# Expert steps for half-full positions: the turn of h and the gate's ScalarE and VectorE work moved to fixed places

## The chip, the cores and the metric

The kernel runs on one core of a Trainium2 chip. The metric is the device time of one execution in microseconds (us), the median of three runs. One execution was also recorded by the hardware profiler; the rows below are from that trace. Its engines are TensorE (PE, with its weight loads as PEld), VectorE (DVE), ScalarE (ACT), GpSimd (POOL) and SyncE (SP), which issues the loads from HBM.

## The reference

A two-layer encoder trunk on 256 tokens of width 1024, all in float32. The change lies in the last block of the second layer, a mixture of eight experts of which each token uses two:

```
def swiglu(xn, w_gu, w_down):
    g, u = jnp.split(xn @ w_gu, 2, axis=-1)
    return (jax.nn.silu(g) * u) @ w_down
...
    for e in range(N_EXPERTS):
        out = out + comb[..., e:e + 1] * swiglu(xn, w_gu[e], w_down[e])
```

An expert's inner width is 3584, so `w_gu` is 1024 x 7168 and `w_down` 3584 x 1024, for each of eight experts.

## The kernel before

The experts are handled one after the other in eight positions. Which expert stands in which position is decided on the chip by the number of its tokens. Positions 2, 4 and 6 (`NARROW`) take at most 64 tokens, the others up to 128. All positions read the same amount of weights.

A position has seven steps j, each for 512 columns of the inner width. A step works on chunks of weights of 128 x 2048 float32 (1.05 MB, one load each): two for the gate (g0, g1), two for the up product (u0, u1), and, from j = 1 on, two for the down product of the step before (d0, d1). Float32 is kept through a split: `split` (L168, L169) makes of a chunk a high part `hi` (a cast on ACT) and a rest `lo` (a subtraction on DVE, which reads `hi`), in two casts of 1024 columns per engine and chunk. `hi` and `lo` rotate through four tiles each, so a cast waits until PE has done with the tile of four casts earlier.

In a narrow position the 64 tokens' high and low parts stand side by side as the 128 columns that PE holds (`xg`, and `ht` for h), so a chunk needs eight matmuls (`narrow`, L1123): four with `hi`, four with `lo`. u1 is not split: four float32 matmuls on the raw chunk (L1139, eight records in the trace). The product then holds two halves of rows that must be added: `gate` copies them crosswise out of PSUM (ACT, L1156, L1157, tile `esg`), adds (DVE, L1158), applies silu (ACT, L1159) and multiplies by the up product (DVE, L1163, tile `eh`), which needs the last u1 matmul. `to_rows` then turns h by four matmuls (L1172, tile `ht`; "the turn" below) and splits it into the side-by-side form (`side_by_side`: ACT L1053, DVE L1054).

Each engine runs its own instructions in order. The order is made by a scheduler from the program's order and the times that it assumes; two instructions of one engine are tied by hand only where `tc.issue_after(ins)` stands. Loads are issued on SP's queue, each as soon as its buffer (11 of `raw`, 6 of `spare`) is free; nothing in the change touches their order.

Of the kernel before, what the change touches and what calls it, by code (L numbers as in the profile page):

```python
# [25 lines left out]
F32 = mybir.dt.float32  # L26
F32R = mybir.dt.float32r
I32 = mybir.dt.int32
AF = mybir.ActivationFunctionType
# [3 lines left out]
P = 128  # L33
D = 1024
KD = D // P
# [4 lines left out]
NE = 8  # L40
# [9 lines left out]
HALF = CAP // 2  # L50
# [31 lines left out]
def _build(ctx, tc, io, cap):  # L82
# [8 lines left out]
    w2b, w1b = 4, 5  # L91
# [8 lines left out]
    def f32(ap):  # L100
        return ap.bitcast(F32)
# [4 lines left out]
    def acc_tile(name="acc"):  # L106
        return psA.tile([P, 512], F32, tag="acc", name=name)
# [4 lines left out]
    def tr_tile(name="tr", dt=F32):  # L112
        return psT.tile([P, 512], dt, tag="tr", name=name)
# [33 lines left out]
            nc.sync.dma_start(raw[:, sl], ap[:, sl])  # L147
        return raw

    done = []  # L150

    def split(raw, n=CH, pieces=2, apart=()):

        cut = (n // 2 + P - 1) // P * P
        parts = []
        for a, b in ((0, cut), (cut, n)):
            if len(parts) in apart:  # L160
                both = rawp.tile([P, CH], F32R, tag="raw", name="apart")
                hi, lo = both[:, :CH // 2], both[:, CH // 2:]
            else:
                hi = hip.tile([P, CH // 2], F32R, tag="hi", name="hi")
                lo = lop.tile([P, CH // 2], F32R, tag="lo", name="lo")
            step = (b - a) * 2 // pieces
            for i in range(0, b - a, step):
                done[:] = (S.copy(hi[:, i:i + step], raw[:, a + i:a + i + step]),  # L168
                           V.tensor_sub(lo[:, i:i + step], raw[:, a + i:a + i + step],  # L169
                                        f32(hi[:, i:i + step])))  # L170
            parts.append((hi, lo))

        def at(a, b):
            hi, lo = parts[a >= cut]
            o = cut if a >= cut else 0
            return hi[:, a - o:b - o], lo[:, a - o:b - o]
        return at
# [620 lines left out]
    last = conv31(KD - 1)  # L798
# [250 lines left out]
    def side_by_side(dst, src):  # L1049

        v = dst.rearrange("p (k s n) -> p k s n", s=2, n=HALF)
        src = src.rearrange("p (k n) -> p k n", n=HALF)
        S.copy(v[:, :, 0, :], src)  # L1053
        V.tensor_sub(v[:, :, 1, :], src, f32(v[:, :, 0, :]))  # L1054

    class Gather:
# [20 lines left out]
        def rows_narrow(self):  # L1077
            px = tr_tile("gx")
            for k in range(KD):
                for t in range(2):  # L1080
                    PE.matmul(px[:, k * HALF:(k + 1) * HALF],
                              xt[:, t * D + k * P:t * D + (k + 1) * P],
                              self.oh[:, t, :HALF], start=t == 0, stop=t == 1)
            side_by_side(xg[:, :D], px)
# [25 lines left out]
    def whole_chunk():  # L1110
        if not ahead:
            fetch()
        return ahead.popleft()

    def chunk(pieces=2):
        return split(whole_chunk(), pieces=pieces)

    def narrow(ps, xs, ws, first, last):

        n = len(xs)  # L1120
        for part in range(2):
            for i, (x, w) in enumerate(zip(xs, ws)):
                ins = PE.matmul(ps, x, w[part], start=first and i == part == 0,  # L1123
                                stop=last and part == 1 and i == n - 1)
        return ins

    def expert(e, g, following):
        nonlocal fn
        py = out_tiles()
        two = e in NARROW  # L1130

        def gate_up(j, gu):
            pz = acc_tile("gu")
            for kh in range(2):
                xs = [xg[:, k * P:(k + 1) * P] for k in range(kh * 4, kh * 4 + 4)]
                if two and gu == kh == 1:
                    w = whole_chunk()
                    for kk in range(4):
                        PE.matmul(pz, f32(xs[kk]), w[:, kk * 512:(kk + 1) * 512],  # L1139
                                  start=False, stop=kk == 3)  # L1140
                    continue
                w = chunk()
                ws = [w(kk * 512, (kk + 1) * 512) for kk in range(4)]
                if two:
                    narrow(pz, xs, ws, kh == 0, kh == 1)
                    continue
                moving(pz, [(xg[:, k * P:(k + 1) * P], xg[:, D + k * P:D + (k + 1) * P])
                            for k in range(kh * 4, kh * 4 + 4)],
                       ws, kh == 0, kh == 1)
            return pz  # L1150

        def gate(pg, pu):
            sg = work.tile([P, 512], F32, tag="w2", name="esg", bufs=w2b)
            if two:

                S.copy(sg[:HALF], pg[HALF:])  # L1156
                S.copy(sg[HALF:], pg[:HALF])  # L1157
                V.tensor_add(sg, sg, pg)  # L1158
                S.activation(sg, sg, AF.Silu, scale=g.cw[:, 1:2])  # L1159
            else:  # L1160
                S.activation(sg, pg, AF.Silu, scale=g.cw[:, 1:2])
            h = work.tile([P, 512], F32, tag="w2", name="eh", bufs=w2b)
            V.scalar_tensor_tensor(h, pu, g.cw[:, 1:2], sg, op0=ALU.mult, op1=ALU.mult)  # L1163
            return h

        def to_rows(j, h):
            pt = tr_tile("ht")
            o = (j % 2) * D
            if two:

                for i in range(4):
                    PE.matmul(pt[:, i * HALF:(i + 1) * HALF], h[:, i * P:(i + 1) * P], both,  # L1172
                              start=True, stop=True)
                return side_by_side(ht[:, o:o + 512], pt[:, :4 * HALF])
            for i in range(4):
                PE.transpose(pt[:, i * P:(i + 1) * P], h[:, i * P:(i + 1) * P], ident)
            S.copy(ht[:, o:o + 512], pt)
            V.tensor_sub(ht[:, o + 512:o + D], pt, f32(ht[:, o:o + 512]))

        def down(j, n):  # L1180
            w = chunk(4 if e == NE - 1 and j == 6 else 2)
            o = (j % 2) * D
            if two:
                return narrow(py[n], [ht[:, o + f * P:o + (f + 1) * P] for f in range(4)],
                              [w(f * 512, (f + 1) * 512) for f in range(4)], j == 0, j == 6)
            return moving(py[n],
                   [(ht[:, o + f * P:o + (f + 1) * P], ht[:, o + 512 + f * P:o + 512 + (f + 1) * P])
                    for f in range(4)],
                   [w(f * 512, (f + 1) * 512) for f in range(4)], j == 0, j == 6)

        def weighted(n):
            src = py[n]
            hi, lo = (work.tile([P, 512], F32R, tag="w2", name=name, bufs=w2b) for name in ("yh", "yl"))
            S.activation(hi, src, AF.Copy, scale=g.cw[:, 0:1])
            done[:] = [V.scalar_tensor_tensor(lo, src, g.cw[:, 0:1], f32(hi),
                                              op0=ALU.mult, op1=ALU.subtract)]
            return hi, lo

        def scatter(n, y, tile=tr_tile):
            for t in range(2):  # L1200
                pz = tile("so")
                PE.matmul(pz, g.oT[:, t * P:(t + 1) * P], y[0], start=True, stop=False)
                PE.matmul(pz, g.oT[:, t * P:(t + 1) * P], y[1], start=False, stop=True)
                a = acc[:, t * D + n * 512:t * D + (n + 1) * 512]
                V.tensor_add(a, a, pz)  # L1205

        h = None
        for j in range(7):
            pg = gate_up(j, 0)
            if j:  # L1210
                to_rows(j - 1, h)
            pu = gate_up(j, 1)
            h = gate(pg, pu)
            if j:
                down(j - 1, 0)
                if j == 6:
                    to_rows(6, h)
                down(j - 1, 1)
            if following is not None and j in (3, 5):
                following.step(j)  # L1220
        if following is not None:
            following.rows()
        else:
            fn = big_tile("fn")
            nc.sync.dma_start(fn[:, :D], io["final_norm"].to_broadcast([P, D]))
        down(6, 0)
        y = weighted(0)
        last = down(6, 1)
        if following is not None:
            scatter(0, y)  # L1230
            scatter(1, weighted(1))
        else:
            y1 = weighted(1)
            with tc.issue_after(last.ins):
                scatter(0, y)
            scatter(1, y1, acc_tile)
# [268 lines left out]
```

## Time and profile before

| | us |
|---|---|
| median of 3 runs (lowest, highest) | 1547.98 (1547.81, 1549.23) |
| the profiled execution | 1547.42 |
| its span in the trace | 1545.7 |
| PE busy | 1511.9 |
| DVE busy | 1298.9 |
| ACT busy | 1052.1 |

The span is the time from the first to the last instruction; the execution's own time is 1.7 us more. Matmuls are pipelined: the record of a 128x512 matmul is 0.39 us long while the next one starts 0.23 us after it, so a busy PE can still have lost time.

### The profile page before, as it was taken

Reading aid. Unit: us, or ns where it says so; the run is one execution under the profiler, and the core shown is the slowest. Engines: PE = TensorE matmul, PEld = TensorE weight load, DVE = VectorE, ACT = ScalarE, POOL = GpSimd, SP = SyncE. Lnnn points to the kernel's source line nnn. Section 1 sums busy time; section 2 is a strip of 40 time slices with the busy share of each in tenths; the row PEclk is TensorE's granted clock in tenths of the full one; section 3 lists DMA queues with packets and bytes.
Section 4 is the critical chain, followed back from the end, with each engine's and each line's share of the span. In section 5 each row is a group of like instructions: output and inputs, shape, how many; then the busy total and the mean of one; then the engine's idle time right before and its main releaser. Section 6 shows DMA issues by size and latency. Waiting matters only on the chain.

```text
span 1545.7 us, 23643 instructions
## 1 busy us (share of the span) xinstructions
PE 1511.9 (98%) x8558; PEld 1294.3 (84%) x8558; DVE 1298.9 (84%) x1735; ACT 1052.1 (68%) x1381; POOL 148.1 (10%) x230
## 2 busy tenths in 40 slices
PE   8999999999999999999999999999999999999996
PEld 8899999999998998888888768888667888667885
DVE  7876677776898868999999989889889888889897
ACT  6555554455585647777777877777777777777775
POOL 4710100001394210000000000000000000000000
PEclk9999999999999999999999999999999999999998
DMA  9654454336536566998999999998999999999950
GB/s 370 269 191 164 142 186 166 120 113 236 188 134 244 174 264 221 371 377 334 373 366 342 397 422 412 381 375 331 403 402 376 367 361 343 408 392 382 364 191 30
DMA packets 65213, 451.42 MB, mean 292 GB/s; under 512 B 7360, under 2 KB 7488, under 8 KB 12480
## 3 DMA queue, kind: packets, MB, share of 16 engines
q1 hardware_dynamic: 65088, 449.83, 76.6%
q8 instruction: 69, 1.13, 0.3%
q14 instruction: 56, 0.46, 0.1%
HBM read 448.75 MB, written 1.05 MB: 291 GB/s over the span
## 4 chain that ended last, share of the span: by engine, by line
PE 82%; DVE 9%; POOL 3%; issue 3%; ACT 2%; DMA 1%; SPq 0%; DVEq 0%; POOLq 0%; ACTq 0%
PE gu L211 8%; PE gu L212 8%; PE gu L216 8%; PE acc L205 7%; PE acc L203 7%; PE acc L204 7%; DVE lo L169 6%; PE gu L1139 5%; PE gu L1123 4%; PE py L211 4%; PE py L216 4%; PE py L212 4%; PE py L1123 3%; POOL part L779 2%; PE gx L1042 1%
## 5 line engine op out<-in xcount | busy, mean ns | idle before, releaser
L169 DVE TENSOR_TENSOR lo<-raw,hi 128x1024 fp32r<-128x1024 f32 (+3 forms) x573 | 671.6, 1208 | 113.9 <-ACT hi L168 103.6
L168 ACT CAST hi<-raw 128x1024 fp32r<-128x1024 f32 (+3 forms) x573 | 565.4, 1030 | 212.9 <-PE acc L204 89.4
L169 DVE TENSOR_TENSOR lo<-spare,hi 128x1024 fp32r<-128x1024 f32 (+1 forms) x226 | 260.9, 1198 | 24.4 <-ACT hi L168 20.4
L168 ACT CAST hi<-spare 128x1024 fp32r<-128x1024 f32 (+1 forms) x226 | 221.5, 1035 | 23.6 <-PE gu L212 11.7
L211 PE MATMUL gu<-hi,xg 128*128 128x512 f32 x560 | 218.8, 391 | 0.0
L212 PE MATMUL gu<-hi,xg 128*128 128x512 f32 x560 | 218.3, 390 | 0.0
L216 PE MATMUL gu<-lo,xg 128*128 128x512 f32 x560 | 154.2, 391 | 0.6 <-DVE lo L169 0.6
L216 PEld LDWEIGHTS gu<-lo,xg 128*128 128x128 f32 x560 | 104.7, 188 | 23.9 <-DVE lo L169 1.9
L211 PEld LDWEIGHTS gu<-hi,xg 128*128 128x128 f32 x560 | 105.1, 188 | 22.2 <-ACT hi L168 0.2
L212 PEld LDWEIGHTS gu<-hi,xg 128*128 128x128 f32 x560 | 105.1, 188 | 21.8
L211 PE MATMUL py<-hi,ht 128*128 128x512 f32 x280 | 111.1, 398 | 0.0
L212 PE MATMUL py<-hi,ht 128*128 128x512 f32 x280 | 109.3, 390 | 0.0
L205 PE MATMUL acc<-a2h,lo 128*128 128x256 f32 x336 | 95.2, 283 | 0.0
L204 PE MATMUL acc<-a2l,hi 128*128 128x256 f32 x336 | 95.2, 283 | 0.0
L203 PE MATMUL acc<-a2h,hi 128*128 128x256 f32 x336 | 95.1, 283 | 0.0
L1401 POOL TENSOR_TENSOR fo<-accum,fn 128x512 f32<-128x512 f32 x2 | 2.5, 1272 | 948.9 <-DVE accum L1205 948.9
L1123 PE MATMUL gu<-lo,xg 128*128 128x512 f32 x252 | 80.4, 411 | 7.9 <-DVE lo L169 7.6
L216 PE MATMUL py<-lo,ht 128*128 128x512 f32 x280 | 84.0, 395 | 0.0
L1123 PE MATMUL gu<-hi,xg 128*128 128x512 f32 x252 | 71.3, 397 | 0.0
L1123 PEld LDWEIGHTS gu<-lo,xg 128*128 128x128 f32 x252 | 43.4, 188 | 31.5 <-DVE lo L169 25.2
L203 PEld LDWEIGHTS acc<-a2h,hi 128*128 128x128 f32 x336 | 64.5, 192 | 0.0
L205 PEld LDWEIGHTS acc<-a2h,lo 128*128 128x128 f32 x336 | 64.5, 192 | 0.0
(424 smaller groups left out, 3171.9 us busy)
## 6 DMA issues: line engine op xcount, KB each, us to landing
raw<-in_moe_gu SPq DMA_DIRECT2D x139, 1024.0 KB, 7.1
spare<-in_moe_gu SPq DMA_DIRECT2D x85, 1024.0 KB, 7.2
raw<-in_moe_down SPq DMA_DIRECT2D x78, 1024.0 KB, 7.4
spare<-in_moe_down SPq DMA_DIRECT2D x32, 1024.0 KB, 7.0
raw<-in_ffn_gu SPq DMA_DIRECT2D x22, 1024.0 KB, 4.8
raw<-in_pw SPq DMA_DIRECT2D x12, 1024.0 KB, 4.8
raw<-in_ffn_down SPq DMA_DIRECT2D x16, 704.0 KB, 4.1
raw<-in_wk SPq DMA_DIRECT2D x8, 1024.0 KB, 7.3
```

What stands on the lines that cost most here:

```text
L168: done[:] = (S.copy(hi[:, i:i + step], raw[:, a + i:a + i + step]), V.tensor_sub(lo[:, i:i + step], raw[:, a + i:a + i + step], f32(hi[:, ...
L169: V.tensor_sub(lo[:, i:i + step], raw[:, a + i:a + i + step], f32(hi[:, i:i + step])))
L203: PE.matmul(ps, a[0], b[0], start=first, stop=False)
L204: PE.matmul(ps, a[0], b[1], start=False, stop=False)
L205: PE.matmul(ps, a[1], b[0], start=False, stop=last)
L211: PE.matmul(ps, a[0], b[0], start=first and i == 0, stop=False)
L212: PE.matmul(ps, a[1], b[0], start=False, stop=False)
L216: ins = PE.matmul(ps, a[0], b[1], start=False, stop=last and i == n - 1)
L779: G.tensor_add(part, part, prod)
L1042: PE.matmul(px[:, kk * P:(kk + 1) * P], xt[:, t * D + d0:t * D + d0 + P], oh[:, t, :], start=t == 0, stop=t == 1)
L1123: ins = PE.matmul(ps, x, w[part], start=first and i == part == 0, stop=last and part == 1 and i == n - 1)
L1139: PE.matmul(pz, f32(xs[kk]), w[:, kk * 512:(kk + 1) * 512], start=False, stop=kk == 3)
```

## The change

For narrow positions a step is written out as a whole (`step_narrow`). The chunks are split in the order g0, g1, u0, d0, d1. The turn of the step before's h is tied behind g0's matmuls, and g1's matmuls behind the turn. The gate's copies and their sum (`fold`) are tied behind the last casts or the last but one, the silu and the multiplication behind the casts of d1; the split of the turned h behind the casts of u0. `casts` only records the ACT instructions to tie to. No instruction is added or taken away; wide positions keep their code.

```diff
-    done = []
+    done, casts = [], []
...
+                casts.append(done[0])
...
+        def step_narrow(j, h):
...
+            pg, pu = acc_tile("gu"), acc_tile("gu")
+            g0 = chunk()
+            g1 = chunk()
+            last = narrow(pg, xs[:4], parts(g0), True, False)
+            u0 = chunk()
+            if j:
+                with tc.issue_after(last.ins):
+                    pt, last = turn_narrow(j - 1, h)
+                with tc.issue_after(casts[-1].ins):
+                    rows_narrow(j - 1, pt)
+            with tc.issue_after(last.ins):
+                narrow(pg, xs[4:], parts(g1), False, True)
+            u1 = whole_chunk()
+            d0 = chunk() if j else None
+            narrow(pu, xs[:4], parts(u0), True, False)
+            d1 = chunk() if j else None
+            with tc.issue_after(casts[-2 if j else -1].ins):
+                sg = fold(pg)
+            for kk in range(4):
+                last = PE.matmul(pu, f32(xs[4 + kk]), u1[:, kk * 512:(kk + 1) * 512],
+                                 start=False, stop=kk == 3)
+            with tc.issue_after(casts[-1].ins):
+                h = gate(sg, pu)
+            if j:
+                down(j - 1, 0, d0)
+                down(j - 1, 1, d1)
+            return h
```

`turn_narrow` holds the four matmuls of the turn, `rows_narrow` the call of `side_by_side`, and `fold` the two copies and the sum that stood in `gate`.

The order that comes out, first on ACT, one step in the middle of position 4 before (the casts are those of d0 and d1 of the step before, then of g0, g1 and u0 of the next step):

```order
L1156 COPY esg<-gu 64x512
L1157 COPY esg<-gu 64x512
L1159 ACTIVATE esg<-esg,cw 128x512
L168 CAST hi<-spare 128x1024 x2
L168 CAST hi<-raw 128x1024 x2
L1053 CAST ht<-ht 128x4x64
L168 CAST hi<-raw 128x1024 x6
```

and now, from the casts of d0 and d1 on:

```order
L168 CAST hi<-spare 128x1024 x2
L168 CAST hi<-raw 128x1024 x2
L1146 COPY esg<-gu 64x512
L1147 COPY esg<-gu 64x512
L168 CAST hi<-raw 128x1024 x2
L1204 ACTIVATE esg<-esg,cw 128x512
L168 CAST hi<-raw 128x1024 x4
L1054 CAST ht<-ht 128x4x64
```

The copies and the silu stood ahead of the four casts of the down chunks; the copies now stand behind them, and the silu behind two casts more (those of the next step's g0).

DVE at the same place before; the two groups of four between `esg` and `ht` are the rests of d0 and d1, the six those of g0, g1 and u0:

```order
L1158 TENSOR_TENSOR esg<-esg,gu 128x512
L169 TENSOR_TENSOR lo<-spare,hi 128x1024
L1163 SCALAR_TENSOR_TENSOR eh<-gu,cw,esg 128x512
L169 TENSOR_TENSOR lo<-spare,hi 128x1024
L169 TENSOR_TENSOR lo<-raw,hi 128x1024 x2
L1054 TENSOR_TENSOR ht<-ht 128x4x64
L169 TENSOR_TENSOR lo<-raw,hi 128x1024 x6
```

and now:

```order
L1148 TENSOR_TENSOR esg<-esg,gu 128x512
L169 TENSOR_TENSOR lo<-raw,hi 128x1024 x2
L1206 SCALAR_TENSOR_TENSOR eh<-gu,cw,esg 128x512
L169 TENSOR_TENSOR lo<-raw,hi 128x1024 x4
L1055 TENSOR_TENSOR ht<-ht 128x4x64
L169 TENSOR_TENSOR lo<-spare,hi 128x1024 x2
L169 TENSOR_TENSOR lo<-raw,hi 128x1024 x2
```

The multiplication that makes h (`eh`) stood inside the four rests of d0 and d1; it now stands behind all four and behind the next step's two of g0.

PE in position 4 before, from the four u1 matmuls on, through d0 and d1 (`py`) and the next step's g0, g1 and u0:

```order
L1139 MATMUL gu<-spare,xg 128x512 x4
L1123 MATMUL py_11128<-hi,ht 128x512 x4
L1123 MATMUL py_11128<-lo,ht 128x512 x2
L1172 MATMUL ht<-kept,eh 128x64 x4
L1123 MATMUL py_11129<-hi,ht 128x512 x2
L1123 MATMUL py_11128<-lo,ht 128x512 x2
L1123 MATMUL py_11129<-hi,ht 128x512 x2
L1123 MATMUL py_11129<-lo,ht 128x512 x4
L1123 MATMUL gu<-hi,xg 128x512 x4
L1123 MATMUL gu<-lo,xg 128x512 x4
```

and now:

```order
L1193 MATMUL gu<-raw,xg 128x512 x4
L1124 MATMUL py_11129<-hi,ht 128x512 x4
L1124 MATMUL py_11129<-lo,ht 128x512 x4
L1124 MATMUL py_11130<-hi,ht 128x512 x4
L1124 MATMUL py_11130<-lo,ht 128x512 x4
L1124 MATMUL gu<-hi,xg 128x512 x4
L1124 MATMUL gu<-lo,xg 128x512 x4
L1155 MATMUL ht<-kept,eh 128x64 x4
L1124 MATMUL gu<-hi,xg 128x512 x4
L1124 MATMUL gu<-lo,xg 128x512 x4
```

The turn moved from 6 matmuls behind u1 to 24 behind it. At a narrow position's last step no g0 follows, and the turn stands straight behind the 16 matmuls of d0 and d1. The steps of positions 4 and 6 read alike, before and now.

## Rows read from the trace of the kernel before

**Rows 1.** The page, part 1: busy time, share of the span, instructions.

```profile
PE 1511.9 (98%) x8558; PEld 1294.3 (84%) x8558; DVE 1298.9 (84%) x1735; ACT 1052.1 (68%) x1381; POOL 148.1 (10%) x230
```

**Rows 2.** Timeline, PE: start, us, instruction; turns in positions 2, 4, 6.

```profile
862.53 1.00 PE L1172 MATMUL ht<-kept,eh 128*128 128x64 f32 x8
...
902.89 1.00 PE L1172 MATMUL ht<-kept,eh 128*128 128x64 f32 x8
...
1086.65 1.00 PE L1172 MATMUL ht<-kept,eh 128*128 128x64 f32 x8
...
1164.75 1.00 PE L1172 MATMUL ht<-kept,eh 128*128 128x64 f32 x8
...
1321.55 1.00 PE L1172 MATMUL ht<-kept,eh 128*128 128x64 f32 x8
...
1399.62 1.00 PE L1172 MATMUL ht<-kept,eh 128*128 128x64 f32 x8
```

**Rows 3.** Stretches from turn to turn: length, busy by engine, PEclk, DMA share, GB/s.

```profile
876.43:889.89 13.46, 13.46 (x58) 9.92 (x56) 13.06 (x14) 11.95 (x15) 0.00 (x0) 1.00 1.00 405
889.89:902.89 13.00, 13.00 (x56) 9.54 (x54) 12.97 (x14) 10.99 (x14) 0.00 (x0) 1.00 1.01 423
...
914.29:929.84 15.55, 14.70 (x57) 9.53 (x56) 13.11 (x14) 11.73 (x14) 0.00 (x0) 1.00 1.01 422
...
1102.21:1117.79 15.58, 14.72 (x58) 9.53 (x56) 13.13 (x14) 11.73 (x14) 0.00 (x0) 1.00 1.01 416
...
1133.33:1149.22 15.89, 15.18 (x64) 10.23 (x63) 13.31 (x15) 12.00 (x15) 0.00 (x0) 1.00 1.00 404
```

**Rows 4.** Timeline of ACT in position 4, a step; brackets: idle before, releaser.

```profile
1095.33 0.58 ACT L1156 COPY esg<-gu 64x512 f32<-64x512 f32 x1 [1.57 <-PE gu L1123]
...
1097.41 0.72 ACT L1159 ACTIVATE esg<-esg,cw 128x512 f32<-128x512 f32 x1 [0.91 <-DVE esg L1158]
1098.04 1.97 ACT L168 CAST hi<-spare 128x1024 fp32r<-128x1024 f32 x2
...
1103.51 5.79 ACT L168 CAST hi<-raw 128x1024 fp32r<-128x1024 f32 x6
```

**Rows 5.** Timeline of DVE in the same step of position 4.

```profile
1099.09 1.23 DVE L169 TENSOR_TENSOR lo<-spare,hi 128x1024 fp32r<-128x1024 f32 x1 [1.72 <-ACT hi L168]
1101.04 0.75 DVE L1163 SCALAR_TENSOR_TENSOR eh<-gu,cw,esg 128x512 f32<-128x512 f32 x1 [0.72 <-PE gu L1139]
1101.70 1.22 DVE L169 TENSOR_TENSOR lo<-spare,hi 128x1024 fp32r<-128x1024 f32 x1
...
1105.44 6.89 DVE L169 TENSOR_TENSOR lo<-raw,hi 128x1024 fp32r<-128x1024 f32 x6
```

**Rows 6.** Timeline of PE: position 4, and the wide position 3's first step.

```profile
1107.84 0.73 PE L1123 MATMUL gu<-lo,xg 128*128 128x512 f32 x2 [0.41 <-DVE lo L169]
...
1112.38 0.74 PE L1123 MATMUL gu<-lo,xg 128*128 128x512 f32 x2 [0.16 <-DVE lo L169]
1112.96 3.60 PE L1139 MATMUL gu<-raw,xg 128*128 128x512 f32 x8
1116.00 1.49 PE L1123 MATMUL py<-hi,ht 128*128 128x512 f32 x4
...
950.24 0.73 PE L216 MATMUL gu<-lo,xg 128*128 128x512 f32 x2 [0.19 <-DVE lo L169]
```

**Rows 7.** The chain in order of time, position 2: start, us, what.

```profile
855.13 3.43 PE gu L1139 x8
858.56 3.67 PE py L1123 x16
...
862.69 0.84 PE ht L1172 x8
```

**Rows 8.** SP's waits (total, times, longest), and loads' us from issue to landing, 830 to 940.

```profile
SPq L147 <- DVE lo L169: 835.4, 307, 14.6
...
DMA to landing us min/median/max: 4.7/12.5/14.3
```

More of the change, by code (lines that the diff above doesn't have):

```diff
@@ L1134, in gate_up @@
             for kh in range(2):
[L1135 to L1141, printed above, removed]
                 w = chunk()
                 ws = [w(kk * 512, (kk + 1) * 512) for kk in range(4)]
-                if two:
-                    narrow(pz, xs, ws, kh == 0, kh == 1)
-                    continue
                 moving(pz, [(xg[:, k * P:(k + 1) * P], xg[:, D + k * P:D + (k + 1) * P])
@@ L1150, in gate_up, with fold @@
             return pz
-        def gate(pg, pu):
[L1153 to L1161, printed above, removed]
+        def fold(pg):
+            sg = work.tile([P, 512], F32, tag="w2", name="esg", bufs=w2b)
+            S.copy(sg[:HALF], pg[HALF:])
+            S.copy(sg[HALF:], pg[:HALF])
+            V.tensor_add(sg, sg, pg)
+            return sg
@@ new lines, in turn_narrow, with rows_narrow, parts @@
+        def turn_narrow(j, h):
+            pt = tr_tile("ht")
+            for i in range(4):
+                ins = PE.matmul(pt[:, i * HALF:(i + 1) * HALF], h[:, i * P:(i + 1) * P], both,
+                                start=True, stop=True)
+            return pt, ins
+        def rows_narrow(j, pt):
+            o = (j % 2) * D
+            side_by_side(ht[:, o:o + 512], pt[:, :4 * HALF])
+        def step_narrow(j, h):
+            xs = [xg[:, k * P:(k + 1) * P] for k in range(KD)]
+            tiles = [(f * 512, (f + 1) * 512) for f in range(4)]
+            def parts(w):
+                return [w(*sl) for sl in tiles]
+            pg, pu = acc_tile("gu"), acc_tile("gu")
[25 more added lines that the diff above has]
+            return h
@@ L1162, in gate @@
+        def gate(pg, pu):
+            sg = pg if two else work.tile([P, 512], F32, tag="w2", name="esg", bufs=w2b)
+            S.activation(sg, pg, AF.Silu, scale=g.cw[:, 1:2])
             h = work.tile([P, 512], F32, tag="w2", name="eh", bufs=w2b)
@@ L1169, in to_rows @@
             if two:
[L1171 to L1174, printed above, removed]
+                return rows_narrow(j, turn_narrow(j, h)[0])
             for i in range(4):
@@ L1178, in to_rows, with down @@
             V.tensor_sub(ht[:, o + 512:o + D], pt, f32(ht[:, o:o + 512]))
-        def down(j, n):
-            w = chunk(4 if e == NE - 1 and j == 6 else 2)
+        def down(j, n, w=None):
+            if w is None:
+                w = chunk(4 if e == NE - 1 and j == 6 else 2)
             o = (j % 2) * D
@@ L1208, in expert @@
         for j in range(7):
+            if two:
+                h = step_narrow(j, h)
+                if j == 6:
+                    to_rows(6, h)
+                if following is not None and j in (3, 5):
+                    following.step(j)
+                continue
             pg = gate_up(j, 0)
```

## Prediction

> **What bounds the kernel now.** I read the page first: PE is busy for 98% of the span and DVE for 84% [rows 1], so the kernel as a whole is PE's, and a change of order can only win where PE waits. The change touches the three narrow positions alone, so the next view is the timeline of PE there, from one turn to the next, which is a step. From the turn at 862.53 to that at 902.89 in position 2 three steps took 40.36 us, 13.45 each [rows 2], and PE has no gap in them [rows 3]. From 1086.65 to 1164.75 in position 4 five steps took 78.10 us, and from 1321.55 to 1399.62 in position 6 five took 78.07 [rows 2]; a plain one is 15.55 [rows 3] (one of each five also holds the next position's `oT` and `cw` work and takes 15.89). One more such step, 914.29 to 929.84, ends position 2. These steps issue the same matmuls. So eleven steps (1 + 5 + 5) are each 15.55 - 13.45 = 2.10 us longer than PE's own work, by the order alone. That PE's own work is 13.4 is seen in the chain too: 16 matmuls of two chunks take 3.67, so five split chunks 9.18, the u1 matmuls 3.43, the turn 0.84 [rows 7], in all 13.45.
>
> Why the slow ones are slow: DVE is busy for 13.13 of 15.58 [rows 3] and idle twice: 1.72 before the first rest of d0, waiting for ACT's cast, and 0.72 before `eh`, waiting for the last u1 matmul [rows 5]; 13.13 + 1.72 + 0.72 = 15.57, the whole step. ACT's cast is late because ahead of it in the queue stand the copies, which waited 1.57 for the gate's last matmul, and the silu, which waited 0.91 for DVE's sum [rows 4]. So the casts of d0 and d1, which need nothing from the gate, queue behind the gate, DVE falls behind, and PE then waits for rests of g0, g1 and u0 (0.41, 0.16, ... [rows 6]; these idle times are shorter than the loss, as a record runs 0.16 beyond the next start and a pair after a wait takes 0.73 where one without takes 0.61). The loop DVE, u1, `eh`, DVE sets the step.
>
> **The change, part by part.** Nothing is added: 40 + 4 + 4 matmuls, ten casts, ten rests, the gate's six instructions, as before. Three things move.
>
> Casts of d0 and d1 ahead of the copies and the silu. This takes away both idle times of DVE: the four casts wait only for tiles that PE frees while it does u0. Worth up to 1.72 + 0.72 = 2.44 per slow step on DVE, of which PE can use 2.10.
>
> `eh` behind the next step's two rests of g0. This is the added wait, and what counts is whether h is ready for the turn. I set t = 0 at the end of the u1 matmuls. PE's four `hi` matmuls of d0 end 0.93 later (1116.00 + 1.49 against 1112.96 + 3.60 [rows 6]), the first pair of them at 0.46. That frees the tile for ACT's cast of g0: 1.05 us, so to 1.55 (six casts take 5.79, two 1.97, so 0.95 from start to start [rows 4]). DVE's two rests start at 1.6 and 2.73 (six take 6.89, one 1.22: 1.134 apart [rows 5]), `eh` at 3.87, done at 4.62 (0.75 [rows 5]); the silu stands behind the second cast, from 2.55 to 3.27, in time. PE arrives at the turn after 24 matmuls, 3.67 x 1.5 = 5.50. The turn has 0.9 us to spare: no wait in a step.
>
> The turn and `ht` queue ahead of g1. Queued behind `eh` on DVE are four rests (g1, u0). `eh` lets the next start after 0.66, at 4.53 [rows 5], so they start at 4.53, 5.66, 6.80, 7.93; the last is done at 9.15. PE wants it for its last u0 pair at 5.50 + 0.84 + 3.67 - 0.46 = 9.55: 0.4 to spare. If it came late, the DVE loop would be 9.15 + 0.46 + 3.43 = 13.04, or 13.2 with a restart: not above PE's 13.45. DVE as a whole needs 12.97 to 13.13 per step [rows 3], also below. So a step becomes PE's 13.45, and the three limits lie within half a microsecond of each other.
>
> The last step of each position has no g0 ahead of the turn: PE is there at 3.67, `eh` done at 4.62; with the hand-over and a restart of 0.12 (0.73 - 0.61) a wait of 1.0 to 1.2, three times. I take 1.2, in all 3.6. It can't be below nothing; where the casts come 0.5 later it is 1.7 each, 5.1.
>
> Edges. Each wide position behind a narrow one now has one wait in its first step, 0.19 of idle [rows 6], with the 0.16 and the 0.12 some 0.47, which the new order of the gathering may take away: 0 to 1.4 in all. The first turn of a narrow position moves ahead of up to eight matmuls, at 0.229 each 1.8 us: bounds of a loss 0 to 1.8, for position 2 alone, as in 4 and 6 it moved by two. I take a gain of 1.0 for the edges, between -1.8 and 1.4 nearer the upper.
>
> Sum: 11 x 2.10 = 23.1 gained, 3.6 given back, 1.0 at the edges: 20.5. From the profiled execution's 1547.42 that is 1526.9; the median of the runs is 0.56 above it, so 1527.5.
>
> **Loads.** A shorter step asks more of the DMA engines: six loads of 1.049 MB in 13.45 us are 468 GB/s, and they deliver 422 or 423 at a share of 1.01 [rows 3], which reads as their limit. The lack is (468 - 422) x 13.45 us = 0.62 MB per step, 0.6 of a load. SP's loads wait for buffers that DVE frees, 307 times [rows 8], so the loads run as far ahead as 17 buffers allow: 17 / 6 x 13.45 = 38 us. Position 2's fast steps ran that way, and the loads landed 14.3 us after issue at the worst [rows 8]. Two steps more add 1.2 loads, 3 us. 38 us cover that, and wide positions need less. So I cost it at nothing.
> The Trainium skill's page "DMA: Bandwidth & Descriptors" (Where 436 GB/s comes from) says that for loads from HBM the HBM side, about 358 GB/s for a core, is what binds. By that, an estimate, six loads take 6.29 MB / 358 GB/s = 17.6 us, more than the step has now, and the change would gain nothing. The stretches of the trace at 405 to 423 GB/s say otherwise for this core.
>
> **Rivals.**
> 1. DVE's loop becomes the bound. The loop above is 13.04 with instructions 1.134 apart; if none overlapped, its six rests cost 1.22 each and `eh` 0.75: 0.6 more, with a restart and hand-overs 14.0. For it: half a microsecond decides. Against: rows of six in a run. Time: 11 x 1.55 = 17.1, less 3.6, plus 1.0, 14.5: 1533.5.
> 2. Loads become the bound, when the lead of 17 is used up: 6.29 MB at 422 GB/s is 14.9 us a step, so 11 x 0.65 = 7.2 - 3.6 + 1.0 = 4.6: 1543.4. At the 404 GB/s of the slow steps it is 15.57, and the change gains nothing: 1548. For it: a DMA share of 1.0. Against: 14.3 us of landing in 38.
> 3. The other side: the turn waits. It stands in front of g1 and everything after it; before, PE had 6 matmuls behind u1 and found `eh` ready. If `eh` were done not at 4.62 but behind the rests of g1 and u0 as well, at 9.2, PE would wait 3.7 at each turn and a step last 13.45 + 3.7 + 0.1 = 17.3: 11 x 1.75 + 2.6 = 21.9 slower, 1570. It decides where `eh` is done later than 5.50 + 2.10 = 7.6. Against: the order has two rests ahead of it, not six.
> 4. It does nothing: the step is held at 15.55 by something that no wait shows. Against: the same matmuls ran at 13.45 in position 2. 1548.
>
> **Chances.** The forecast 0.78 (1523.5 to 1530.5: three limits this close move 11 steps by 0.1 to 0.2 at most, 2 us; last turns and edges 3); rival 1 0.11; rival 2 0.05 with a gain, 0.02 without; rival 3 0.02; rival 4 0.02. A measurement of this kernel tells 0.2%, 3 us. Faster: 0.78 + 0.11 + 0.05 = 0.94. Same 0.04, slower 0.02. The range 1523.5 to 1533.5 holds the forecast and most of rival 1, some 0.85.
>
> **What would show it.** Turn to turn 13.3 to 13.6 in positions 4 and 6; PE without a wait for `lo` there, and one of about 1 us at the last turn; ACT casting d0 and d1 while PE does u0 and u1; DVE idle under 0.5 a step; GB/s above 420 and landing up to 18 us in these positions. Wrong if a step stays above 13.8, if the turn waits in every step, or if ACT waits for a load.

## The result, and the profile after

The changed kernel took 1528.15 us (median of four runs, 1527.87 to 1528.61) against 1548.61 (1547.81 to 1549.54) for the kernel before in the same session: a ratio of 0.987, 95% interval 0.9858 to 0.9882. The profiled execution took 1527.87 us, its span is 1526.1. The forecast was 1527.5, and 1526.9 for the profiled execution, so the gain is 19.55 us there where 20.5 were forecast; between the two medians it is 20.46.

The page after, the line of busy time that answers to [rows 1]:

```profile
PE 1499.1 (98%) x8558; PEld 1298.5 (85%) x8558; DVE 1302.1 (85%) x1735; ACT 1056.3 (69%) x1381; POOL 148.1 (10%) x230
```

DVE and ACT have the same work as before; they only do it at another time. Where the time went is read from PE's turns, the answer to [rows 2] (start, us, instruction; in brackets the idle time before and what ended it). Three of positions 4 and 6 each, the first, the sixth and the last:

```profile
1076.15 1.00 PE L1155 MATMUL ht<-kept,eh 128*128 128x64 f32 x8
...
1144.20 1.00 PE L1155 MATMUL ht<-kept,eh 128*128 128x64 f32 x8
1157.04 1.10 PE L1155 MATMUL ht<-kept,eh 128*128 128x64 f32 x8 [1.00 <-DVE eh L1206]
...
1301.78 1.00 PE L1155 MATMUL ht<-kept,eh 128*128 128x64 f32 x8
...
1369.78 1.00 PE L1155 MATMUL ht<-kept,eh 128*128 128x64 f32 x8
1382.61 1.11 PE L1155 MATMUL ht<-kept,eh 128*128 128x64 f32 x8 [1.00 <-DVE eh L1206]
```

Five steps of position 4 take 68.05 us (1076.15 to 1144.20) where they took 78.10, and those of position 6 take 68.00 where they took 78.07. Only the last turn of each waits. The stretches from turn to turn, as in [rows 3] (length, busy time by engine, granted clock, DMA share, GB/s):

```profile
1103.11:1116.57 13.46, 13.46 (x58) 9.93 (x57) 13.00 (x14) 11.60 (x15) 0.00 (x0) 1.00 1.02 421
...
1130.05:1144.20 14.15, 14.15 (x64) 10.55 (x62) 13.18 (x15) 11.88 (x16) 0.00 (x0) 1.00 1.01 421
```

PE is busy over the whole length of both; plain steps take 13.45 to 13.50. The second holds the next position's `oT` and `cw` work.

The queues that made the old step long look like this now, ACT first, one step of position 4 (answers to [rows 4]):

```profile
1104.85 2.01 ACT L168 CAST hi<-spare 128x1024 fp32r<-128x1024 f32 x2
1106.76 2.00 ACT L168 CAST hi<-raw 128x1024 fp32r<-128x1024 f32 x2
1108.78 0.58 ACT L1146 COPY esg<-gu 64x512 f32<-64x512 f32 x1
...
1111.77 2.00 ACT L168 CAST hi<-raw 128x1024 fp32r<-128x1024 f32 x2 [1.82 <-PE py L1124]
1113.67 0.72 ACT L1204 ACTIVATE esg<-esg,cw 128x512 f32<-128x512 f32 x1
```

The casts of d0 and d1 (the first two rows) run without a wait, and when the copies and the silu come up their inputs are long there. ACT still waits 1.82 us in the step, but now for the tile of g0's cast, which PE frees in its first matmuls of d0; PE never waits for it. DVE in the same step (answers to [rows 5]):

```profile
1112.86 2.36 DVE L169 TENSOR_TENSOR lo<-raw,hi 128x1024 fp32r<-128x1024 f32 x2 [0.46 <-ACT hi L168]
1115.14 0.74 DVE L1206 SCALAR_TENSOR_TENSOR eh<-gu,cw,esg 128x512 f32<-128x512 f32 x1
```

DVE's idle time in a step is 0.46 where it was 1.72 + 0.72. PE (answers to [rows 6]):

```profile
1107.68 3.59 PE L1193 MATMUL gu<-raw,xg 128*128 128x512 f32 x8
...
1116.57 1.00 PE L1155 MATMUL ht<-kept,eh 128*128 128x64 f32 x8
```

With the end of the u1 matmuls as zero (1107.68 + 3.59 = 1111.27), `eh` is done at 4.61 (1115.14 + 0.74) and PE comes to the turn at 5.30. All of PE's waits from 540 us to the end, and then, from the trace of the kernel before, its waits for rests in the same part:

```profile
PE ht L1155 <- DVE eh L1206: 3.0, 3, 1.0
PE pp L1013 <- DVE sel L1001: 0.6, 1, 0.6
PE so L1243 <- DVE yl L1235: 0.6, 1, 0.6
PE lead L205 <- DVE ol L270: 0.4, 1, 0.4
```

```profile
PE gu L1123 <- DVE lo L169: 7.6, 31, 0.4
PE gu L216 <- DVE lo L169: 0.6, 3, 0.3
```

The numbers are the total in us, how many times, and the longest. No wait for a `lo` is left, in the wide positions (L216 before) neither. The three waits for `eh` are the last turns, and they are what the change gave back.

### The profile page after: what moved, and what is told of

It is laid out like the page before. It is cut to its first block, busy times and chain, and to the rows that moved or that the text cites. A ratio compares the mean times of both kernels' runs of the same rounds, so it can differ in the third digit from the quotient of the medians.

```text
span 1526.1 us, 23758 instructions
## 1 busy us (share of the span) xinstructions
PE 1499.1 (98%) x8558; PEld 1298.5 (85%) x8558; DVE 1302.1 (85%) x1735; ACT 1056.3 (69%) x1381; POOL 148.1 (10%) x230
## 3 DMA queue, kind: packets, MB, share of 16 engines
q8 instruction: 69, 1.13, 0.3%
## 4 chain that ended last, share of the span: by engine, by line
PE 88%; POOL 4%; DVE 3%; ACT 2%; issue 1%; DMA 1%; SPq 0%; POOLq 0%; DVEq 0%; ACTq 0%
PE gu L217 8%; PE gu L213 8%; PE gu L212 8%; PE gu L1124 7%; PE acc L206 7%; PE acc L205 7%; PE acc L204 7%; PE py L1124 5%; PE gu L1193 4%; PE py L217 4%; PE py L212 4%; PE py L213 4%; POOL part L780 2%; PE ht L1155 1%; PE gx L1043 1%
## 5 line engine op out<-in xcount | busy, mean ns | idle before, releaser
L217 PE MATMUL gu<-lo,xg 128*128 128x512 f32 x560 | 157.3, 392 | 0.0
L217 PEld LDWEIGHTS gu<-lo,xg 128*128 128x128 f32 x560 | 104.8, 188 | 22.0
L1124 PE MATMUL gu<-lo,xg 128*128 128x512 f32 x252 | 70.7, 392 | 0.0
L205 PEld LDWEIGHTS acc<-a2l,hi 128*128 128x128 f32 x336 | 64.6, 192 | 0.0
```

The costliest lines, as they stand in the source:

```text
L205: PE.matmul(ps, a[0], b[1], start=False, stop=False)
L217: ins = PE.matmul(ps, a[0], b[1], start=False, stop=last and i == n - 1)
```

## The experiments

The runs were made on three chips, and each is compared with runs of the kernel before on its own chip (medians 1547.63, 1548.2 and 1547.59 us), so it is the ratios that can be set side by side.

**Which of the moved things made the gain.** My theory was the place of the gate's copies and silu on ACT; the rival was the place of the turn. One run keeps the gate's ties and gives the turn back to the program's order:

```diff
-            if j:
-                with tc.issue_after(last.ins):
-                    pt, last = turn_narrow(j - 1, h)
-                with tc.issue_after(casts[-1].ins):
-                    rows_narrow(j - 1, pt)
-            with tc.issue_after(last.ins):
-                narrow(pg, xs[4:], parts(g1), False, True)
+            narrow(pg, xs[4:], parts(g1), False, True)
+            if j:
+                pt, _ = turn_narrow(j - 1, h)
+                with tc.issue_after(casts[-1].ins):
+                    rows_narrow(j - 1, pt)
```

> The casts of the down chunks stand ahead of the gate's copies and silu as in the change; the turn goes back to the place that the program order gives it, behind or amid the second gate chunk. My theory (the whole gain is the casts of d0 and d1 no longer queueing behind the gate on ACT): steps in positions 4 and 6 stay at 13.4 to 13.5 us turn to turn, total within 3 us of the changed kernel, 1528 to 1531. Rival (the gain comes from the turn standing early, so that the rows of ht are ready early): steps go back towards 15.6, total 1545 to 1549.

Measured: 1529.39 us (1528.88 to 1530.23), ratio 0.9879 (0.9864 to 0.9895). The turn then stands two matmuls into g1, 26 behind u1, not 6 as in the kernel before. Two of PE's turns in position 4:

```profile
1090.87 1.00 PE L1155 MATMUL ht<-kept,eh 128*128 128x64 f32 x8
1104.34 1.00 PE L1155 MATMUL ht<-kept,eh 128*128 128x64 f32 x8
```

A step of 13.47, and an interval that overlaps the change's. The turn's place between the chunks adds nothing to a plain step, once the gate is out of the way. It is not without worth: the `oT` and `cw` work follows the turn, and the step that holds it takes 14.94 in positions 4 and 6 of this run (1131.30 to 1146.24 in position 4), 0.79 more than with the change. The next run does the reverse, the turn's place alone, with the gate, the rows of `ht` and the chunks' splits in the program's order of before:

```diff
-                with tc.issue_after(casts[-1].ins):
-                    rows_narrow(j - 1, pt)
+                rows_narrow(j - 1, pt)
...
-            with tc.issue_after(casts[-2 if j else -1].ins):
-                sg = fold(pg)
...
-            with tc.issue_after(casts[-1].ins):
-                h = gate(sg, pu)
+            sg = fold(pg)
+            h = gate(sg, pu)
...
-                down(j - 1, 0, d0)
-                down(j - 1, 1, d1)
+                down(j - 1, 0)
+                down(j - 1, 1)
```

> The turn stands behind g0 as in the change; the gate, the rows of ht and the casts of the down chunks keep the order of the kernel before, so ACT has the copies and the silu ahead of the casts of d0. My theory: no gain, ACT's casts of d0 wait for the gate and DVE's rests for them; the rows of ht now also stand ahead of a rest on DVE. Steps in positions 4 and 6 15.5 to 16.2 us, total 1548 to 1557. Rival (the turn's place is the gain): 13.5 us a step, total 1528 to 1531.

Measured: 1554.15 us (1553.9 to 1555.37), ratio 1.0042 (1.0027 to 1.0058): slower than the kernel before. Two turns of position 4, and what ACT does behind the first:

```profile
1108.85 1.00 PE L1155 MATMUL ht<-kept,eh 128*128 128x64 f32 x8
1124.91 1.00 PE L1155 MATMUL ht<-kept,eh 128*128 128x64 f32 x8
```

```profile
1109.89 0.37 ACT L1054 CAST ht<-ht 128x256 fp32r<-128x256 f32 x1 [2.79 <-PE ht L1155]
1110.16 2.00 ACT L168 CAST hi<-raw 128x1024 fp32r<-128x1024 f32 x2
```

A step is 16.06. ACT waits 2.79 us for the turn with two casts queued behind it, which is why the change also ties the rows of `ht` behind the casts of u0, and the gate still stands ahead of the casts of d0. So I took back the gate's place and nothing else:

```diff
-            with tc.issue_after(casts[-2 if j else -1].ins):
+            with tc.issue_after(casts[-5 if j else -1].ins):
                 sg = fold(pg)
...
-            with tc.issue_after(casts[-1].ins):
+            with tc.issue_after(casts[-5 if j else -1].ins):
                 h = gate(sg, pu)
```

> As the change, turn and rows of ht where the change has them; the one thing undone is the place of the gate: copies and silu go ahead of the casts of d0 on ACT, as in the kernel before. My theory (that place alone is the gain): DVE is again idle before the first rest of d0, for ACT's cast, and before eh, PE waits for rests, plain steps in positions 4 and 6 15.0 to 15.7 us, total 1542 to 1549. Rival (the gain needs any fixed order, whichever it is, or comes from the turn): 13.45 us, total about 1528.

Measured: 1546.02 us (1545.32 to 1547.59), ratio 0.9989 (0.998 to 0.9999). Two turns, and the first rest of d0 on DVE between them:

```profile
1107.28 1.00 PE L1155 MATMUL ht<-kept,eh 128*128 128x64 f32 x8
1122.52 1.00 PE L1155 MATMUL ht<-kept,eh 128*128 128x64 f32 x8
```

```profile
1113.84 1.23 DVE L169 TENSOR_TENSOR lo<-spare,hi 128x1024 fp32r<-128x1024 f32 x1 [1.72 <-ACT hi L168]
```

The step is 15.24, and the rest has the very idle time of [rows 5], 1.72 us for ACT's cast. Against the runs of its chip this run keeps 1.6 us of a gain of 19.6. With it and the first, the place of the gate (copies, sum, silu and multiplication, moved together) is shown to be the gain; that it acts through ACT's queue is read from the 1.72. The Trainium skill's page "PSUM — Partial Sum Buffer" (Engine vs sequencer instructions) says that the queues of ACT, DVE and POOL are strictly first in, first out; the casts of d0, which had their data and waited behind a copy that had not, agree with it.

**How near the turn is to its limit.** The silu and `eh` are carried into the next step and tied behind the casts of g1, so that four rests stand ahead of `eh` instead of two (the last step keeps the change's order):

```diff
             last = narrow(pg, xs[:4], parts(g0), True, False)
+            if j:
+                with tc.issue_after(casts[-1].ins):
+                    h = gate(*h)
...
-            with tc.issue_after(casts[-1].ins):
-                h = gate(sg, pu)
+            h = (sg, pu)
+            if j == 6:
+                with tc.issue_after(casts[-1].ins):
+                    h = gate(sg, pu)
```

> The silu and eh of a step are carried on and stand behind the casts and rests of the next g1 (four rests ahead of eh instead of two); all else as in the change. My theory (h is done about 0.7 us before PE wants it, and each rest more ahead of eh costs 1.13 us on DVE): eh is done about 2.3 us later, PE waits around the turn in each step but the last of a position, and a step takes 14.5 to 15.1 us instead of 13.45; total 1548 to 1556, the whole gain lost. Rival (h has far more room than that, the turn is not near a limit): steps stay at 13.45, total 1528.

Measured: 1549.2 us (1548.79 to 1550.15), ratio 1.0009 (0.9999 to 1.0018). Two turns of PE, and `eh` between them on DVE:

```profile
1113.95 1.08 PE L1155 MATMUL ht<-kept,eh 128*128 128x64 f32 x8 [0.28 <-DVE eh L1211]
...
1118.13 3.59 PE L1196 MATMUL gu<-raw,xg 128*128 128x512 f32 x8
...
1127.73 0.74 PE L1124 MATMUL gu<-hi,xg 128*128 128x512 f32 x2 [0.56 <-ACT hi L168]
1128.75 0.96 PE L1155 MATMUL ht<-kept,eh 128*128 128x64 f32 x7 [0.28 <-DVE eh L1211]
```

```profile
1127.86 0.74 DVE L1211 SCALAR_TENSOR_TENSOR eh<-gu,cw,esg 128x512 f32<-128x512 f32 x1
```

`eh` is done 6.88 us after the u1 matmuls (1127.86 + 0.74 against 1118.13 + 3.59) instead of 4.61, 2.27 later, and a step takes 14.80, which is 1.34 longer than 13.46. So some 0.9 of the 2.27 was free. The rows of the change give 0.7 between `eh` and the turn; the scheduler here also put two matmuls of u0 ahead of the turn, which wait for ACT, so this run does not settle which it is. The whole gain is lost by putting the silu and `eh` behind the work of one chunk more, two casts and two rests.

**How much DVE has free.** One or two instructions more on DVE in each narrow step, right behind `eh`, into a tile that nobody reads:

```diff
+            for _ in range(1):
+                x = work.tile([P, 512], F32, tag="w2", name="extra", bufs=w2b)
+                V.tensor_sub(x, sg, sg)
             if j:
                 down(j - 1, 0, d0)
```

> As the change, with one more tensor_sub of 128x512 on DVE in each narrow step, right behind eh, into a tile that nobody reads. A rest of 128x1024 takes 1.13 from start to start in the trace, so this should take 0.55 to 0.70. My theory (DVE is busy for 13.0 of 13.45 and its loop over u1, eh and the rests of g1 and u0 is about as long, so 0.4 to 0.45 us a step is all that is free): a step becomes 13.6 to 14.0, total 1532 to 1539. Rival (DVE's order is what counted and it has room to spare, PE alone sets the step): 13.45 a step, total 1528.

> As the run before with two such instructions, 1.1 to 1.4 us more on DVE in each narrow step. My theory: DVE has 14.1 to 14.4 us of work a step and sets it, 14.2 to 14.6; each step loses about as much more as the second instruction takes, total 1540 to 1551. Rival: 13.45 a step, total 1528 to 1530.

Measured: 1536.67 us (1535.76 to 1537.34), ratio 0.9924 (0.9907 to 0.9941), with one, and 1547.71 (1546.71 to 1549.36), ratio 0.9996 (0.9986 to 1.0006), with two. One step of DVE with one more:

```profile
1103.22 2.36 DVE L169 TENSOR_TENSOR lo<-raw,hi 128x1024 fp32r<-128x1024 f32 x2 [0.32 <-ACT hi L168]
...
1106.15 0.68 DVE L1199 TENSOR_TENSOR extra<-esg 128x512 f32<-128x512 f32 x1
1106.75 1.22 DVE L169 TENSOR_TENSOR lo<-raw,hi 128x1024 fp32r<-128x1024 f32 x1
```

and the stretches of a step, with one and then with two, the second with the rests of g1 and u0 on DVE and the u1 matmuls on PE:

```profile
1092.99:1106.94 13.95, 13.74 (x57) 9.85 (x56) 13.63 (x15) 11.62 (x15) 0.00 (x0) 1.00 1.02 428
```

```profile
1098.39:1112.94 14.55, 14.15 (x58) 9.64 (x56) 14.21 (x16) 11.91 (x15) 0.00 (x0) 1.00 1.00 414
```

```profile
1098.81 4.62 DVE L169 TENSOR_TENSOR lo<-spare,hi 128x1024 fp32r<-128x1024 f32 x4
```

```profile
1104.05 3.60 PE L1193 MATMUL gu<-spare,xg 128*128 128x512 f32 x8
```

The extra instruction holds DVE for 0.60 (1106.15 to 1106.75). The second adds exactly that (14.55 - 13.95), so DVE's loop sets both steps, and without the extra work it is 13.95 - 0.60 = 13.35. PE's 13.46 is only 0.1 above it. Of DVE's idle 0.46 a step, all but 0.1 belongs to the loop: it is the wait for ACT's cast of g0 (0.32 in the first row above), which waits for PE's first matmuls of d0, which stand behind u1.

**How near the loads are to their limit.** Eight buffers of `raw` instead of eleven (`NRAW = 8`), one execution:

> As the change with 8 buffers of the raw pool in place of 11, so that the loads of the expert stage run ahead by 14 loads and not by 17: 14 / 6 x 13.45 = 31 us. The stages ahead of the experts use the same pool and may get slower by tens of microseconds, so it is read by steps, not by the total. My theory (loads take up to 17.6 us from issue to landing in these positions, so the lead is nearly twice what is needed): steps in positions 2, 4 and 6 stay at 13.45, ACT waits for no load. Rival (the loads are on the edge, as DMA engines are busy all the time): steps of 14 us and more in the last steps of a position, ACT or PE waiting for a load there.

Measured: 1591.93 us. Two turns of position 4:

```profile
1153.67 1.00 PE L1155 MATMUL ht<-kept,eh 128*128 128x64 f32 x8
1167.14 1.00 PE L1155 MATMUL ht<-kept,eh 128*128 128x64 f32 x8
```

The plain steps stay at 13.45 to 13.47, a load lands 17.0 us after its issue at the worst, and no engine waits for one there. The 64 us are lost before the experts, where PE waits 38.1 us for the loads of `in_pw`; the last section comes back to that.

**Taking the last turn's wait away.** In the last step no g0 stands ahead of the turn, so the gate is tied two casts earlier there:

```diff
-            with tc.issue_after(casts[-2 if j else -1].ins):
+            with tc.issue_after(casts[-4 if j == 6 else -2 if j else -1].ins):
                 sg = fold(pg)
...
-            with tc.issue_after(casts[-1].ins):
+            with tc.issue_after(casts[-3 if j == 6 else -1].ins):
                 h = gate(sg, pu)
```

> In the last step of each narrow position alone, the copies stand behind the first cast of d0 and the silu and eh ahead of the casts of d1, so that h is done before PE comes to the last turn. My theory (the last turn's wait of 1.0 us, and its restart, are given back by the change): no wait at the last turns, 1.0 to 1.2 us gained at each of three, total 3 to 4 us less than the changed kernel, 1524 to 1525.5. Rival (the casts of d1 then come late and PE waits as long for their rests): 1528, with a wait for a rest of d1 or of the next position's weights in place of the turn's.

Measured: 1524.22 us (1523.82 to 1525.38), ratio 0.9849 (0.9835 to 0.9862). ACT in the last step of position 4, and PE's last two turns:

```profile
1144.60 2.01 ACT L168 CAST hi<-raw 128x1024 fp32r<-128x1024 f32 x2
1146.63 0.58 ACT L1146 COPY esg<-gu 64x512 f32<-64x512 f32 x1
...
1147.83 1.99 ACT L168 CAST hi<-raw 128x1024 fp32r<-128x1024 f32 x2
1149.91 0.72 ACT L1204 ACTIVATE esg<-esg,cw 128x512 f32<-128x512 f32 x1
```

```profile
1142.82 1.00 PE L1155 MATMUL ht<-kept,eh 128*128 128x64 f32 x8
1154.49 1.00 PE L1155 MATMUL ht<-kept,eh 128*128 128x64 f32 x8
```

A tie only says what must stand ahead: the scheduler put the silu behind the casts of d1 all the same, not ahead of them as the expectation says, but ahead of the next casts, so that `eh` comes two rests earlier. The turn waits for nothing, and the last step takes 11.67 instead of 12.84. To compare it with the change itself, both ran again in one session:

> The changed kernel itself once more, on the same chip and against the same runs of the kernel before as the version with the early gate in the last steps, so that the two can be compared: 1527.5 to 1528.7.

> The version with the early gate in the last steps, beside the changed kernel. My theory (a wait of 1.0 us and its restart taken away three times): 3.3 to 4.2 us less than the changed kernel, 1523.8 to 1525. Rival (the gain of the first measurement was a difference of chips): within 1 us of the changed kernel.

Measured: 1528.0 us (1527.43 to 1528.71), ratio 0.9871 (0.9854 to 0.9887), for the change, and 1525.29 (1524.68 to 1525.59), ratio 0.9853 (0.9837 to 0.987), without the last wait. The runs of the two don't overlap (the intervals of the ratios do); 2.7 us apart is less than the 3.3 that I expected at least. By the traces the edit gives 1.2 to 1.3 in each of three positions; the profiled execution of the second came to the first turn of position 2, ahead of anything that the edit touches, 0.69 us later than that of the first (853.04 against 852.35). This version has the lowest ratio of all that ran.

The last question was whether the gate may stand there in every step (`casts[-4]` and `casts[-3]` for all j but the first):

> As the run with the early gate in the last steps, but in every narrow step: copies behind the first cast of d0, silu and eh ahead of the casts of d1. It asks how far behind the gate has to stand. My theory (what the change removes is d0's casts behind the gate; d1's may stand behind it, as PE wants them 1.8 us later): plain steps stay at 13.4 to 13.6 us, total 1524 to 1528, equal to or up to 3 us behind the run with the last steps alone. Rival (all four casts must be ahead of the gate, since each stall of DVE there is lost for the whole step): steps of 14.0 us or more, total above 1533.

Measured: 1526.07 us (1525.24 to 1527.21), ratio 0.9858 (0.9841 to 0.9874). As in the run before, the copies came to stand between the casts of d0 and d1 and the silu behind d1's. Plain steps take 13.45; in the step with the `oT` and `cw` work one wait appears:

```profile
1128.79 1.00 PE L1155 MATMUL ht<-kept,eh 128*128 128x64 f32 x8
1134.27 0.73 PE L1124 MATMUL gu<-lo,xg 128*128 128x512 f32 x2 [0.40 <-DVE lo L169]
1143.75 1.00 PE L1155 MATMUL ht<-kept,eh 128*128 128x64 f32 x8
```

That step takes 14.96 instead of 14.15. So the copies need not stand behind both down chunks; behind d0's casts will do. The silu ended behind d1's here too, so whether it could stand ahead of them is not shown. The order that the change uses has more room in the step with `oT` and `cw`, and this one has no wait at the last turns.

## Why the prediction was right, step by step

- **Eleven slow steps, 2.10 each.** Right in mechanism, a little too large. The five steps of position 4 gave 10.05 and those of position 6 10.07, where 10.5 were forecast. Most of the missing 0.4 is in the step with `oT` and `cw`: it was 0.34 above a plain step before (15.89 against 15.55 [rows 3]) and is 0.69 now (14.15 against 13.46). So its matmuls, which seem to have fallen partly into PE's waits before, now add their whole length.
- **`eh` behind two rests more.** Done at 4.61, forecast 4.62. PE comes at 5.30, not 5.50: the 3.67 of [rows 7] runs to the end of the last matmul's record, and the next matmul starts 0.16 before that end; the forecast's 3.67 x 1.5 didn't take this off. The room is 0.7 instead of 0.9, and no turn between the first and the last of a position waits.
- **The last turns, 1.2 each given back.** Idle 1.00 and with the restart 1.3: the first turn of position 4 came 1.31 earlier (1074.84 against 1076.15) where position 2's last wait was taken away. Three times 1.3 is 3.9 against 3.6.
- **Edges, 1.0 gained.** The waits for a `lo` that ended a wide position's first step are gone. Position 2's slow step can be taken out: from its second u1 matmuls to its last 70.06 us passed before (854.97 to 925.03) and 68.01 do now (855.12 to 923.13), 2.05 less for the 2.10 forecast. What is left for the edges is 19.55 + 3.9 - 20.12 - 2.05 = 1.28; of that, 0.25 is there already at position 2's first u1 matmuls (845.36 against 845.61), ahead of everything that was moved.
- **The bound that comes next.** The three limits were said to lie within half a microsecond: DVE's loop 13.04, or 13.2 with a restart, PE 13.45. The loop was forecast too short; it is 13.35. Its rests were right, its end was not: in the run with two more on DVE 4.22 pass from the end of the last rest to the end of u1 (1098.81 + 4.62 to 1104.05 + 3.60), where 0.46 + 3.43 = 3.89 were put; the other 13.35 - 4.22 = 9.13 stand against 9.15. Rival 1 was 0.1 us away, not 0.25 to 0.4. Its step of 14.0 was priced at 1533.5, over eleven steps; the run with 13.95 took 1536.67, since DVE's loop lengthens all steps of the three positions.
- **Loads at no cost.** Right: 421 GB/s at a share of 1.01 to 1.02 in these steps, no wait for a load, even with three buffers fewer, and in position 4, from issue to landing:

```profile
DMA to landing us min/median/max: 4.6/12.0/17.6
```

  The forecast was up to 18. Rival 2 is out. The rule of the Trainium skill's page "DMA: Bandwidth & Descriptors" (Where 436 GB/s comes from), by which about 358 GB/s from HBM would bind, is not what this one core shows.
- **Rivals 3 and 4.** Rival 3 needs `eh` later than the change has it; with one chunk's work more ahead of it the whole gain went, so it was a matter of the order alone. Rival 4, a step held at 15.55 by something that no wait shows, is out with 13.46.

## What to carry to other kernels

On an engine that works in order, an instruction that must wait holds up everything queued behind it, so work whose data is there (casts of loaded weights) goes ahead of work that waits for a late result; here four casts behind two copies and a silu cost 2.1 us of each 15.55 us step. Before moving a result back, add up what then stands ahead of it and when its reader comes: two rests of 1.13 us were free, and the order that put two more rests, with their casts, ahead lost everything. And look at the ends of a loop by themselves: the last pass, which lacks the cover of the next, gave back about 1.3 us three times until it had an order of its own.

## What the runs showed of the hardware

The loss of 64 us with eight buffers was larger than PE's waits for loads (38.1 us). Stretches of that run (length, busy time of PE, PEld, DVE, ACT, POOL, granted clock, DMA share, GB/s):

```profile
420.00:430.00 10.00, 1.35 (x7) 0.84 (x5) 5.30 (x24) 5.04 (x9) 0.00 (x0) 0.70 0.57 210
430.00:440.00 10.00, 0.00 (x0) 0.00 (x0) 10.00 (x22) 6.03 (x13) 8.41 (x9) 0.50 0.27 89
440.00:450.00 10.00, 8.75 (x32) 7.17 (x32) 8.83 (x23) 0.00 (x0) 0.77 (x2) 0.78 0.04 17
```

While PE stood still from 421 to 441 us its granted clock went to 0.50, the lower of its two levels (1.2 and 2.4 GHz), and over the 10 us from 440 on, of which PE was busy for 8.75, the mean was 0.78. What part of the 64 us this makes was not measured by itself. In the narrow steps, where PE never pauses, the clock stays at 1.00.
